# A four-layer decoder trunk on one core: the feed forward's gate and up by tokens in 512 columns, and all weight splits on VectorE

## The chip, the core and the metric

The kernel runs on one core of one Trainium2 chip. A core has TensorE (PE, matrix products into PSUM), VectorE (DVE), ScalarE (ACT), GpSimd (POOL) and SyncE (SP, which here issues the loads), each with its own instruction stream; they meet through semaphores. The metric is the device time of one execution in microseconds, the median of several runs.

## The reference

Input x has 256 tokens of width 1024, c is one conditioning vector. Four layers follow each other. Each has a token mixer (sliding window attention, gated linear attention, forgetting attention, sliding window again) and a feed forward of inner width 2816, both behind an RMS norm whose shift, scale and gate come from c:

```python
for i in range(DEPTH):                        # 4
    mod = silu(c) @ ada_w[i] + ada_b[i]       # 6 vectors of 1024
    sh1, sc1, g1, sh2, sc2, g2 = jnp.split(mod, 6, axis=-1)
    h = modulate(rmsnorm(x, norm_gain[i, 0]), sh1, sc1)
    x = x + g1[:, None, :] * mixer(h)
    h = modulate(rmsnorm(x, norm_gain[i, 1]), sh2, sc2)
    g, u = jnp.split(h @ ffn_w_gu[i], 2, axis=-1)
    x = x + g2[:, None, :] * ((silu(g) * u) @ ffn_w_down[i])
return rmsnorm(x, final_norm)
```

All data are float32. One pass over the weights, some 296 MB, is read from HBM.

## The kernel before

**Layout.** x, h and the inner activation lie with features on the 128 partitions and the 256 tokens along the free dimension: x is 8 tiles of 128 features, the inner activation 22 (FT). S is 256, P is 128, KT is 8, NB is 2 blocks of 128 tokens.

**Three products for one.** Products run in float32r, a shorter format at a higher pace. To keep float32's precision each operand is split in two parts, hi = round(v) and lo = v - hi, and `mm3` (L258) makes a product from three: hi x hi, hi x lo, lo x hi (L260, L261, L262). A weight's first part wh is a cast on ScalarE (L195), its second part wl a subtraction (L197) on VectorE, or on GpSimd for the pieces that `on_pool` lists. An activation is split in the same way by `split_hl` (L491: cast at L493, subtraction at L494).

**The stream of weights.** `Stream` (L76) holds all matrices in the order of use. Each is one load of 1 MB (a down weight 0.7 MB) into one of five raw buffers (RAW), issued on SP when the matrix five places ahead has been worked off and its readers are done. A "w" matrix is split in `cuts` pieces (four: 512 columns, or 352 of a down weight); an "a" matrix, a quarter of a modulation vector's matrix, is multiplied with silu(c) and summed on VectorE in two steps of 1024 columns (L217). The builder places this work between the products: `start_chunk` (L222) divides the pieces that are due by the ticks of the chunk, and each `tick` emits its share, up to two weights ahead (LOOK). The layer below fixes each engine's order when the program is built, by its own estimate of what is ready; at run time every engine then goes through its list in that order and stands still where the next instruction waits.

**Who splits.** `MIX_POOL`, `OUT_POOL` and `FFN_POOL` (L55, L62, L63) give one of a weight's four pieces to GpSimd in most stages, two in layer 2's mixer.

**The feed forward** (`ffn`, L1029). Gate and up: 22 weights a layer, each 128 gate columns beside 128 up columns, "by features": the weight is PE's stationary operand, h's 256 tokens stream by. A weight is a chunk of 16 x 3 = 48 products of 256 columns. The first chunk (`first_chunk`, L447) starts from x before the norm is known. Then ScalarE makes silu(g) (L1044), VectorE multiplies by u (L1045), ScalarE casts the result to ah (L493), GpSimd subtracts to al (L494). PSUM's "mm" banks (three) are used in turn, so PE can be two chunks ahead of the activation. Down: for each of 8 output tiles m two weights (11 tiles of depth each), 22 x 3 products of 256 columns into one accumulator; then `add_x` (L496) adds it to x, times the gate, on VectorE, and `x_done` (L400) prepares the next norm. Between the gate/up weights come four vectors' modulation matrices (16 loads; in layer 3 one vector's, 4 loads), between the down weights four loads more (not in layer 3).

Of the kernel before, what the change touches and what calls it, by code (L numbers as in the profile page):

```python
# [10 lines left out]
F32R = mybir.dt.float32r  # L11
# [6 lines left out]
P = 128  # L18
# [36 lines left out]
MIX_POOL = ((0,), (0,), (0, 1), (2,))  # L55
# [5 lines left out]
CUTS = (4, 4, 4)  # L61
OUT_POOL = (1,)  # L62
FFN_POOL = (3,)  # L63
# [12 lines left out]
class Stream:  # L76
    """Matrices in the order of use: each is loaded once; a weight is then split into two float32r
    parts, a modulation matrix multiplied with c. The work on them is cut into pieces, which the
    builder places between the products of the chunks before."""
# [19 lines left out]
    def piece(self):  # L99
        """Emit the next piece, unless it would run too far ahead."""  # L100
# [43 lines left out]
class Builder:  # L144
# [56 lines left out]
    def ada_pieces(self, it, raw):  # L201
        """Two tiles of 128 columns of c_act @ ada_w + ada_b."""
# [61 lines left out]
    def banks(self, split):  # L264
        """Two accumulators: in one bank, one after the other, or side by side in two."""
# [9 lines left out]
    def proj_feat(self, w, hs, split=None):  # L275
        """[cols, tokens]: weights stationary, two tiles of 128 columns."""
# [13 lines left out]
    def proj_tok(self, w, hs, split=None):  # L290
        """[tokens, 256 cols] for both blocks of tokens: activations stationary."""
# [13 lines left out]
    def stat_start(self, acc):  # L305
        """The means of squares, but for the last tile's."""
# [5 lines left out]
    def stat_end(self, acc=None):  # L312
        """1/sqrt(mean + eps) of each token: a column for each block of tokens."""
# [14 lines left out]
    def spread(self, y):  # L328
        """A row of the tokens' values in all partitions, in PSUM."""
# [6 lines left out]
    def rsqrt(self, y, ms):  # L336
        """y = (ms + eps) ** -0.5 by Newton steps, where another table is in use."""
# [27 lines left out]
    def next_norm(self, layer, sub):  # L365
        """Before the last sums into x: the modulation of the norm that follows."""
# [24 lines left out]
    def u_space(self, tag, dtype=F32):  # L391
        """The room of u, which is free between a sublayer's first chunk and the next norm."""
# [7 lines left out]
    def x_done(self, m, eng=None):  # L400
        """x's tile m is final: its squares, and its product with the gain in two parts."""
# [99 lines left out]
    def out_proj(self, layer, oh, ol, gate):  # L501
        """The mixer's last product, in two halves of its depth."""
# [179 lines left out]
    def first_chunks(self):  # L682
        """The first chunks of layer 0, k by k as the modulation comes in."""
# [72 lines left out]
    def few_cols(self, parts):  # L756
        """The 16 columns after a chunk's 256, as [16 cols, tokens] in PSUM."""
# [70 lines left out]
    def gla(self, layer, oh, ol, pool):  # L828
# [41 lines left out]
        def decay(h, li):  # L870
            """exp(-|b - b at the end of the even block| / 16) for every token."""
# [157 lines left out]
    def ffn(self, layer):  # L1029
        nc = self.nc  # L1030
        gate = self.mod[layer][:, 5 * KT:6 * KT]
        with self.tc.tile_pool(name=f"ffn{layer}", bufs=1, reuse_waits="tile") as pool:
            ah = self.t(pool, [P, FT, S], "ah", F32R)
# [278 lines left out]
```

## Time and profile before

Three runs took 1326.77 us (median), 1325.36 and 1332.42 us. The profiled execution's span, from the first to the last instruction, is 1324.8 us: 2.0 us under the median.

| stretch of the span | layer 0 | layer 1 | layer 2 | layer 3 |
|---|---|---|---|---|
| mixer, us | 157.4 | 136.7 | 129.1 | 99.2 |
| gate and up, us | 132.8 | 130.6 | 130.8 | 129.6 |
| down, us | 67.1 | 67.3 | 71.3 | 63.9 |

The rest, 9.0 us, is the last norm and the output. Over the span the loads move 224 GB/s; the busiest stage moves 299 GB/s with its 16 DMA engines busy 82% of the time.

How to read the lines that follow. A row of groups or of a line's instructions names line, engine, operation and operands as out<-in; "x600" is a count. A row of the timeline begins with the start in us and the duration in us. Products on PE are pipelined: a row's duration is longer than its share of the time, and the pace is the difference of two starts. In the table by stretches each engine has its busy time in us and, in brackets, its instructions. A row of waits has the sum in us, the number of waits and the longest. PE's weight loads stand apart as PEld. PEclk is the granted share of PE's clock.

### The profile page before, as it was taken

What the parts mean: (1) busy time and instruction counts of PE and PEld (TensorE: products, weight loads), DVE (VectorE), ACT (ScalarE), POOL (GpSimd) and SP (SyncE); (2) the same over time, 40 slices, a digit from 0 to 9 for tenths busy, and PEclk for the clock granted to TensorE, in tenths of its full rate; (3) what the DMA queues carried; (4) which work ended last, traced back from release to release, by engine and by line L of the source; (5) the groups of instructions that cost most, each with busy time, mean ns of one, the idle gap of its engine ahead of it and who ended that gap; (6) DMA issues with size and microseconds to landing.
All of it is one profiled execution on the core that took longest, in us unless ns stands there. A gap on an engine that the chain in (4) does not pass through costs nothing.

```text
span 1324.8 us, 25659 instructions
## 1 busy us (share of the span) xinstructions
PE 1240.9 (94%) x9748; PEld 1182.8 (89%) x9748; DVE 1036.2 (78%) x1959; ACT 756.3 (57%) x1770; POOL 593.3 (45%) x507
## 2 busy tenths in 40 slices
PE   3789899999998899999999999999999999999997
PEld 2666899999998889999999888999988878999997
DVE  5989999985889989897679557999757977744442
ACT  4466754544686656544556766644445667654443
POOL 6467355653435434554345423455434223444431
PEclk9989999999999999999999999999999999999999
DMA  7764679886745336887775443698767533565450
GB/s 313 254 224 159 258 256 333 343 284 238 283 165 180 136 131 243 334 321 266 247 288 182 178 164 123 259 342 321 252 223 284 197 128 119 200 223 201 161 180 33
DMA packets 44702, 298.89 MB, mean 226 GB/s; under 512 B 5169, under 2 KB 5329, under 8 KB 14242
## 3 DMA queue, kind: packets, MB, share of 16 engines
q1 hardware_dynamic: 43778, 295.53, 61.4%
q8 instruction: 76, 1.25, 0.4%
q10 hardware_dynamic: 432, 1.20, 0.2%
q0 software_dynamic: 368, 0.53, 0.2%
q14 instruction: 48, 0.39, 0.1%
HBM read 296.15 MB, written 1.05 MB: 224 GB/s over the span
## 4 chain that ended last, share of the span: by engine, by line
PE 50%; DVE 8%; DMA 3%; issue 2%; ACT 1%; POOL 0%; DVEq 0%; POOLq 0%; ACTq 0%; SPq 0%
PE mm L260 15%; PE mm L261 15%; PE mm L262 15%; DMA raw<-in_ada 3%; DVE wl L197 2%; PE o L551 1%; DVE hl L430 1%; DVE raw L217 1%; PE s L545 1%; DVE tk L435 1%; PE t L585 1%; PE s L544 1%; DVE x L497 1%; PE o L552 1%; DVE ul L419 0%
## 5 line engine op out<-in xcount | busy, mean ns | idle before, releaser
L195 ACT CAST wh<-raw 128x512 fp32r<-128x512 f32 (+1 forms) x816 | 430.2, 575 | 170.6 <-issue 85.0
L197 DVE TENSOR_TENSOR wl<-raw,wh 128x512 fp32r<-128x512 f32 (+2 forms) x600 | 439.6, 768 | 94.3 <-ACT wh L195 92.2
L197 POOL TENSOR_TENSOR wl<-raw,wh 128x512 fp32r<-128x512 f32 (+1 forms) x216 | 321.8, 1492 | 299.6 <-ACT wh L195 277.9
L260 PE MATMUL mm<-hh,wh 128*128 128x256 f32 x1504 | 429.3, 285 | 0.0
L262 PE MATMUL mm<-hh,wl 128*128 128x256 f32 x1504 | 426.5, 284 | 0.0
L261 PE MATMUL mm<-hl,wh 128*128 128x256 f32 x1504 | 426.3, 283 | 0.0
L217 DVE CUSTOM_DVE_ANT_0 raw<-raw,cact,const 128x1024 f32<-128x1024 f32 x174 | 289.7, 1684 | 81.4 <-DMA raw<-in_ada 79.5
L260 PEld LDWEIGHTS mm<-hh,wh 128*128 128x128 f32 x1504 | 289.1, 192 | 1.4 <-issue 1.4
L261 PEld LDWEIGHTS mm<-hl,wh 128*128 128x128 f32 x1504 | 289.2, 192 | 0.4 <-issue 0.3
L262 PEld LDWEIGHTS mm<-hh,wl 128*128 128x128 f32 x1504 | 289.0, 192 | 0.3 <-issue 0.3
L262 PE MATMUL mm<-ah,wl 128*128 128x256 f32 x704 | 200.5, 285 | 12.3 <-DVE wl L197 12.2
L494 POOL TENSOR_TENSOR al<-s,ah 128x256 fp32r<-128x256 f32 x88 | 105.5, 1200 | 227.0 <-ACT ah L493 216.4
L260 PE MATMUL mm<-ah,wh 128*128 128x256 f32 x704 | 200.3, 285 | 0.0
L261 PE MATMUL mm<-al,wh 128*128 128x256 f32 x704 | 199.4, 283 | 0.0
L262 PEld LDWEIGHTS mm<-ah,wl 128*128 128x128 f32 x704 | 133.9, 190 | 13.9 <-DVE wl L197 13.9
L261 PEld LDWEIGHTS mm<-al,wh 128*128 128x128 f32 x704 | 134.3, 191 | 0.0
L260 PEld LDWEIGHTS mm<-ah,wh 128*128 128x128 f32 x704 | 134.1, 190 | 0.0
L493 ACT CAST ah<-s 128x256 fp32r<-128x256 f32 x88 | 35.6, 407 | 125.5 <-DVE s L1045 124.5
L416 POOL TENSOR_TENSOR sq<-sq,sq 128x256 f32<-128x256 f32 x54 | 48.2, 892 | 100.2 <-ACT sq L405 99.0
L260 PE MATMUL mm<-wh,hh 128*128 128x256 f32 x240 | 73.4, 307 | 19.7 <-ACT hh L437 19.7
L405 ACT ACTIVATE sq<-x 128x256 f32<-128x256 f32 x72 | 29.6, 416 | 97.1 <-DVE x L497 95.2
L497 DVE SCALAR_TENSOR_TENSOR x<-mm,mod,x 128x256 f32<-128x256 f32 x96 | 45.7, 478 | 41.2 <-PE mm L262 40.8
(220 smaller groups left out, 2137.1 us busy)
## 6 DMA issues: line engine op xcount, KB each, us to landing
raw<-in_ada SPq DMA_DIRECT2D x96, 1024.0 KB, 6.1
raw<-in_gu SPq DMA_DIRECT2D x88, 1024.0 KB, 5.2
raw<-in_down SPq DMA_DIRECT2D x64, 704.0 KB, 4.9
raw<-in_swa_in SPq DMA_DIRECT2D x12, 1024.0 KB, 7.5
raw<-in_gla_in SPq DMA_DIRECT2D x11, 1024.0 KB, 5.2
raw<-in_fox_in SPq DMA_DIRECT2D x11, 1024.0 KB, 6.7
raw<-in_swa_o SPq DMA_DIRECT2D x8, 1024.0 KB, 4.8
raw<-in_gla_o SPq DMA_DIRECT2D x4, 1024.0 KB, 4.8
```

Source lines behind the costliest of these rows:

```text
L195: nc.scalar.copy(wh[:, sl], raw[:, sl])
L197: eng.tensor_tensor(out=wl[:, sl], in0=raw[:, sl], in1=wh[:, sl].bitcast(F32), op=ALU.subtract)
L217: nc.vector.tensor_tensor_reduce(out=w, in0=w, in1=self.cact, scale=1.0, scalar=b, op0=ALU.mult, op1=ALU.add, accum_out=col)
L260: nc.tensor.matmul(out, ah, bh, start=first, stop=False)
L261: nc.tensor.matmul(out, ah, bl, start=False, stop=False)
L262: nc.tensor.matmul(out, al, bh, start=False, stop=last)
L405: nc.scalar.activation(q, xm, AF.Square)
L416: (eng or nc.gpsimd).tensor_tensor(out=q, in0=self.acc, in1=q, op=ALU.add)
L430: nc.vector.scalar_tensor_tensor(out=hl[:, k], in0=tk, scalar=sh[:, k:k + 1], in1=hh[:, k].bitcast(F32), op0=ALU.add, op1=ALU.subtract)
L493: nc.scalar.copy(hi, src)
L494: (eng or nc.vector).tensor_tensor(out=lo, in0=src, in1=hi.bitcast(F32), op=ALU.subtract)
L497: self.nc.vector.scalar_tensor_tensor(out=self.x[:, m], in0=ps, scalar=gate[:, m:m + 1], in1=self.x[:, m], op0=ALU.mult, op1=ALU.add)
```

## The change

Constants: no piece goes to GpSimd, and a weight is cut in two (pieces of 1024 columns, 704 of a down weight).

```diff
-MIX_POOL = ((0,), (0,), (0, 1), (2,))
+MIX_POOL = ((), (), (), ())
...
-CUTS = (4, 4, 4)
-OUT_POOL = (1,)
-FFN_POOL = (3,)
+CUTS = (2, 2, 2)
+OUT_POOL = ()
+FFN_POOL = ()
```

Gate and up: the first two chunks of a layer stay by features (`gate_up_feat`, with their split on ScalarE and GpSimd). The other 20 weights are laid out anew on the host: two loads of 1 MB, each half of the depth, make a group of 256 gate and 256 up columns. A group goes "by tokens": h is stationary, 512 weight columns stream by, one PSUM bank for each block of 128 tokens. The result has tokens on the partitions, so four transposes on PE bring it back (`turn`); they stand in the program behind the second depth step of the next group, the last group's behind the fourth depth step of the down product.

```diff
+    def gate_up_tok(self, layer, g, pool, a, before):
+        nc = self.nc
+        hh, hl = self.hs
+        outs = [self.ps("s" if g % 2 == 0 else "mm") for _ in range(NB)]
+        for half in range(2):
+            w = self.st.get(f"g{layer}_{2 * g + half}")
+            wh, wl = (x.rearrange("p (k n) -> p k n", k=KT // 2) for x in w)
+            self.start_chunk(KT // 2)
+            for i in range(KT // 2):
+                k = half * (KT // 2) + i
+                for b in range(NB):
+                    sl = slice(b * P, (b + 1) * P)
+                    self.mm3(outs[b], hh[:, k, sl], hl[:, k, sl], wh[:, i], wl[:, i],
+                             k == 0, k == KT - 1)
+                if k == 1 and before is not None:
+                    before()
+                self.tick()
+        s = self.t(pool, [P, NB, 2 * P], "st", bufs=2)
+        for b in range(NB):
+            nc.scalar.activation(s[:, b], outs[b][:, :2 * P], AF.Silu)
+            nc.vector.tensor_tensor(out=s[:, b], in0=s[:, b], in1=outs[b][:, 2 * P:], op=ALU.mult)
+
+        def turn():
+            tp = self.ps("t")
+            for f in range(2):
+                for b in range(NB):
+                    nc.tensor.transpose(tp[:, f * S + b * P:f * S + (b + 1) * P],
+                                        s[:, b, f * P:(f + 1) * P], self.c("ident"))
+            tp = tp.rearrange("p (f n) -> p f n", f=2)
+            self.split_hl(tp, a[:, 2 * g:2 * g + 2, 0], a[:, 2 * g:2 * g + 2, 1])
+        return turn
```

Here `split_hl` has no engine named, so its subtraction, 512 columns from PSUM, is VectorE's.

Down: both parts of the activation lie side by side in one tile `a`, so the weight's first part multiplies both in one product of 512 columns, and its second part the first in one of 256. The accumulator is twice as wide, and its two halves are added to x one after the other.

```diff
-                        self.mm3(o, wh[:, k], wl[:, k], ah[:, kk], al[:, kk], kk == 0, kk == FT - 1)
+                        nc.tensor.matmul(o, wh[:, k], a[:, kk].rearrange("p e n -> p (e n)"),
+                                         start=kk == 0, stop=False)
+                        nc.tensor.matmul(o[:, S:], wl[:, k], a[:, kk, 0], start=False, stop=kk == FT - 1)
+                        if k == 3 and turn is not None:
+                            turn()
+                            turn = None
...
-                self.add_x(m, o, gate)
+                for e in range(2):
+                    self.add_x(m, o[:, e * S:(e + 1) * S], gate)
```

The rest of the diff is the host's layout of the gate/up weights and dropped comments.

More of the change, by code (lines that the diff above doesn't have):

```diff
@@ L1026, in gla, with gate_up_feat @@
         self.bg_rate = GLA_RATE[1]
+    def gate_up_feat(self, layer, j, pool, a):
+        nc = self.nc
+        s = self.t(pool, [P, S], "st", bufs=2)
+        if j == 0:
+            self.hs, ((gv, gc), (uv, uc)) = self.first_chunk(f"g{layer}_0")
+            nc.scalar.activation(s, gv, AF.Silu, bias=gc)
+            nc.vector.scalar_tensor_tensor(out=s, in0=uv, scalar=uc, in1=s, op0=ALU.add, op1=ALU.mult)
+        else:
+            g, u = self.proj_feat(self.st.get(f"g{layer}_{j}"), self.hs, "s")
+            nc.scalar.activation(s, g, AF.Silu)
+            nc.vector.tensor_tensor(out=s, in0=s, in1=u, op=ALU.mult)
+        self.split_hl(s, a[:, j, 0], a[:, j, 1], nc.gpsimd)
+    def gate_up_tok(self, layer, g, pool, a, before):
+        nc = self.nc
+        hh, hl = self.hs
[26 more added lines that the diff above has]
+        return turn
     def ffn(self, layer):
@@ L1032, in ffn @@
         with self.tc.tile_pool(name=f"ffn{layer}", bufs=1, reuse_waits="tile") as pool:
-            ah = self.t(pool, [P, FT, S], "ah", F32R)
-            al = self.t(pool, [P, FT, S], "al", F32R)
-            for j in range(FT):
-                s = self.t(pool, [P, S], "s", bufs=3)
-                if j == 0:
-                    hs, ((gv, gc), (uv, uc)) = self.first_chunk(f"g{layer}_0")
-                    nc.scalar.activation(s, gv, AF.Silu, bias=gc)
-                    nc.vector.scalar_tensor_tensor(out=s, in0=uv, scalar=uc, in1=s, op0=ALU.add,
-                                                   op1=ALU.mult)
-                else:
-                    g, u = self.proj_feat(self.st.get(f"g{layer}_{j}"), hs, "s" if j == 1 else None)
-                    nc.scalar.activation(s, g, AF.Silu)
-                    nc.vector.tensor_tensor(out=s, in0=s, in1=u, op=ALU.mult)
-                self.split_hl(s, ah[:, j], al[:, j], nc.gpsimd)
-                if layer == 0 and j == 2:
+            a = self.t(pool, [P, FT, 2, S], "a", F32R)
+            for j in range(2):
+                self.gate_up_feat(layer, j, pool, a)
+            turn = None
+            for g in range(1, FT // 2):
+                turn = self.gate_up_tok(layer, g, pool, a, turn)
+                if layer == 0 and g == 1:
                     self.late_loads()
-                elif layer == 0 and j == 9:
+                elif layer == 0 and g == 4:
                     self.late_consts()
@@ L1052, in ffn @@
             for m in range(KT):
-                o = self.ps("mm")[:, :S]
+                o = self.ps("mm")
                 for hf in range(2):
@@ L1059, in ffn @@
                         kk = hf * nk + k
-                        self.mm3(o, wh[:, k], wl[:, k], ah[:, kk], al[:, kk], kk == 0, kk == FT - 1)
+                        nc.tensor.matmul(o, wh[:, k], a[:, kk].rearrange("p e n -> p (e n)"),
[3 more added lines that the diff above has]
+                            turn()
+                            turn = None
                         if k % 2:
@@ L1237, in _layout @@
     a["ada"] = ada.reshape(DEPTH * 6, 4, 2, P, D).transpose(0, 1, 3, 2, 4).reshape(DEPTH * 6, 4, P, 2 * D)
-    gu = i["ffn_w_gu"].reshape(DEPTH, KT, P, 2, FT, P)
-    a["gu"] = gu.transpose(0, 4, 2, 1, 3, 5).reshape(DEPTH, FT, P, KT * 2 * P)
+    gu = i["ffn_w_gu"].reshape(DEPTH, KT, P, 2, FT, P)[:, :, :, :, :2]
+    gu = gu.transpose(0, 4, 2, 1, 3, 5).reshape(DEPTH, 2, P, KT * 2 * P)
+    gt = i["ffn_w_gu"].reshape(DEPTH, 2, KT // 2, P, 2, FT // 2, 2 * P)[:, :, :, :, :, 1:]
+    gt = gt.transpose(0, 5, 1, 3, 2, 4, 6).reshape(DEPTH, FT - 2, P, KT * 2 * P)
+    a["gu"] = np.concatenate([gu, gt], 1)
     dn = i["ffn_w_down"].reshape(DEPTH, 2, FT // 2, P, KT, P)
```

## The prediction

> **What bounds the kernel now.** I read the page's busy times and its chain first, then the busy times stretch by stretch, with the borders at the first product of each feed forward (first chunk), of each down product and of each mixer.
>
> ```profile
> PE 1240.9 (94%) x9748; PEld 1182.8 (89%) x9748; DVE 1036.2 (78%) x1959; ACT 756.3 (57%) x1770; POOL 593.3 (45%) x507
> ```
> ```profile
> PE 50%; DVE 8%; DMA 3%; issue 2%; ACT 1%; POOL 0%; DVEq 0%; POOLq 0%; ACTq 0%; SPq 0%
> ```
> ```profile
> core 0: us, PE busy (x) PEld busy (x) DVE busy (x) ACT busy (x) POOL busy (x), PEclk, DMA share, GB/s
> 0.00:157.40 157.40, 115.79 (x697) 93.37 (x698) 133.12 (x271) 94.11 (x231) 91.88 (x86) 0.97 0.65 245
> 157.40:290.20 132.80, 129.36 (x1070) 128.32 (x1069) 130.48 (x185) 68.86 (x152) 74.66 (x49) 1.00 0.82 299
> 290.20:357.30 67.10, 63.45 (x530) 62.84 (x529) 47.09 (x79) 34.18 (x82) 25.75 (x24) 1.00 0.74 259
> 357.30:494.00 136.70, 125.71 (x993) 121.24 (x992) 122.64 (x285) 94.49 (x200) 58.26 (x56) 0.99 0.45 159
> 494.00:624.60 130.60, 129.29 (x1070) 128.27 (x1069) 117.72 (x177) 67.88 (x146) 65.86 (x44) 1.00 0.78 294
> 624.60:691.90 67.30, 64.97 (x530) 64.55 (x529) 47.09 (x83) 34.58 (x83) 26.21 (x24) 0.97 0.73 254
> 691.90:821.00 129.10, 125.92 (x961) 114.81 (x960) 88.60 (x206) 93.08 (x241) 56.05 (x50) 1.00 0.48 167
> 821.00:951.80 130.80, 129.35 (x1070) 128.32 (x1069) 118.22 (x177) 67.82 (x147) 67.22 (x44) 1.00 0.79 293
> 951.80:1023.10 71.30, 65.02 (x531) 64.42 (x530) 47.23 (x83) 34.36 (x83) 26.13 (x24) 0.98 0.69 240
> 1023.10:1122.30 99.20, 97.68 (x698) 83.15 (x697) 84.15 (x235) 67.35 (x181) 27.71 (x47) 1.00 0.43 153
> 1122.30:1251.90 129.60, 128.79 (x1071) 128.30 (x1069) 72.59 (x130) 66.86 (x147) 53.82 (x45) 1.00 0.55 197
> ```
>
> Half of the chain is PE, and in the four gate/up stages (132.8, 130.6, 130.8, 129.6 us) PE is busy but for 1 to 3 us. VectorE (DVE) runs beside it and is nearly full in layer 0 (130.5 of 132.8 us), yet without stopping PE. The down stages lose 2 to 6 us each. So in the feed forwards a shorter PE stream is worth its full length, as long as VectorE keeps up; the waits show where it doesn't:
>
> ```profile
> ACT ah L493 <- DVE s L1045: 124.5, 62, 6.0
> ...
> DVE raw L217 <- DMA raw<-in_ada: 79.5, 24, 6.1
> ...
> PEld mm L262 <- DVE wl L197: 13.9, 8, 3.3
> ```
>
> PE itself waits only 13.9 us for split weights, all of it in products with wl, behind modulation loads that VectorE waited for. But ScalarE waits 124.5 us for VectorE's s: VectorE is late, and so far nobody on PE minds.
>
> **The pace of a product.** The next rows give start times of PE's products.
>
> ```profile
> 229.75 0.28 PE L260 MATMUL mm<-hh,wh 128*128 128x256 f32 x1
> ...
> 235.51 0.28 PE L260 MATMUL mm<-hh,wh 128*128 128x256 f32 x1
> ...
> 699.02 0.28 PE L260 MATMUL s<-wh,hh 128*128 128x272 f32 x1
> ...
> 703.52 0.29 PE L260 MATMUL s<-wh,hh 128*128 128x272 f32 x1
> ```
> ```profile
> 358.79 0.47 PE L309 MATMUL t<-const,sq 128*128 128x1 f32 x3
> 359.12 0.58 PE L322 MATMUL t<-const,sq 128*128 128x1 f32 x4
> ...
> 749.21 0.28 PE L262 MATMUL mm<-hh,wl 128*128 128x256 f32 x1
> 749.33 0.49 PE L585 MATMUL t<-const,pr 128*128 128x128 f32 x3
> 749.57 0.37 PE L260 MATMUL mm<-hh,wh 128*128 128x256 f32 x1
> 749.78 0.28 PE L261 MATMUL mm<-hl,wh 128*128 128x256 f32 x1
> ```
>
> A chunk's 48 products of 256 columns take 5.76 us: 120 ns each. Thirty-six products of 272 columns take 4.50 us: 125 ns each. One-column products go 0.33 us for three, 110 ns each: that is what a change of weights costs with nothing to stream, so a good part of the 120 ns is a load that a longer stream could hide. Three transposes between two products: from 749.21 to 749.78 are 570 ns where two products alone would take 240, so 330 ns, 110 ns a transpose.
>
> No product of 512 columns of this type is in the trace. Ends: if all 120 ns go by columns, 240 ns; if only the growth from 256 to 272 columns counts (5 ns for 16), 120 + 256 x 0.31 = 199 ns. The slope hangs on 5 ns and the proportional end on nothing being fixed, so I take the middle, a little to the long side: 222 ns.
>
> The Trainium skill, TensorE: Matmul & The Clock Gate, section Back-to-back issue gap, gives the spacing as N / 2.4 plus 2.5 ns, 216 ns at 512 columns. The same rule gives 109 ns at 256, where the trace shows 120, so it is short here by 11. By 216 the sum below would be about 15 us lower.
>
> **The change, part by part.**
>
> *Gate and up.* Of 22 weights a layer 20 go by tokens: 20 x 48 x 4 = 3840 products of 256 columns become 1920 of 512. Gain 1920 x (240 - 222) = 34.6 us (0 to 79 by the ends). Added on PE: four transposes for each of 10 groups in 4 layers, 160 x 0.110 = 17.6 us, all on the path, since PE is the bound. The rows above show one transpose alone to last 0.27 us (0.49 for three less two steps of 0.11); in the stream only its 0.11 counts. The loads stay the same in number, size and queue; a group now fills two PSUM banks at once, "mm" and "s" in turn, and "s" is otherwise idle there.
>
> The Trainium skill, same page, section Part 4: PE-mode transpose, speaks against this step: it gives about 275 ns for a transpose in a kernel. By that the 160 would cost 44 us, not 17.6, and the sum would lose all its gain; the trace's 110 ns in the stream of products contradicts it here.
>
> *Down.* Three products of 256 become one of 512 and one of 256, 704 times: 704 x 18 = 12.7 us (0 to 29). Each sum into x is now two steps of VectorE; inside the stage the next tile's products hide the second, at the end of a layer nothing does.
>
> ```profile
> L197 DVE TENSOR_TENSOR wl<-raw,wh x600: 507/679/4459, 17.6 to 1305.4; 128x512 fp32r<-128x512 f32 x101, 128x352 fp32r<-128x352 f32 x48, 128x544 fp32r<-128x544 f32 x1
> ```
> ```profile
> L217 DVE CUSTOM_DVE_ANT_0 raw<-raw,cact,const x174: 1256/1286/3396, 14.8 to 1229.0; 128x1024 f32<-128x1024 f32 x174
> ```
> ```profile
> L1045 DVE TENSOR_TENSOR s<-s,mm x80: 405/410/420, 184.3 to 1253.0; 128x256 f32<-128x256 f32 x80
> ```
> ```profile
> L497 DVE SCALAR_TENSOR_TENSOR x<-mm,mod,x x96: 467/479/486, 121.5 to 1316.1; 128x256 f32<-128x256 f32 x96
> ```
>
> These are min/median/max in ns. Four layer ends x 0.4 us (0.479 less an overlap of 0.08): +1.6 us.
>
> *The split on VectorE alone.* A piece of 512 costs 0.679 us, one of 352 0.507: 1.08 ns a column, so a piece of 1024 about 1.23 us. A weight costs VectorE 2.46 us, where it paid three pieces, 2.04 us, and GpSimd the fourth. But these prices are of undisturbed steps: the maxima (4459 and 3396 ns) are steps that run beside GpSimd, while L1045, which reads one input from PSUM, is never stretched (405 to 420). GpSimd loses its split pieces and nearly all L494 pieces, so most of the stretching goes. A group (two weights) in layers 0 to 2 then asks of VectorE: four pieces 4.92, 1.6 modulation matrices of two steps 1.6 x 2 x 1.29 = 4.1, two products with s 0.82, the new split from PSUM 0.41 + 256 x 1.08 ns = 0.69: 10.5 us, near 10 with the 0.08 us by which following steps overlap (0.68 at 593.97, below, and the next 0.60 later). PE needs 48 x 0.222 + 0.44 = 11.1 us. VectorE fits, with a tenth to spare; layer 3 has a quarter of the matrices. ScalarE has fewer, longer casts and no longer waits for s.
>
> *Waits removed and added.* A raw buffer is given back to SP when its last reader is done; GpSimd's late pieces no longer hold it, so modulation loads are issued sooner. I take half of PE's 13.9 us as gone: -6 us (0 to -13). The added wait is PE's own: the transposes need s, and behind them in PE's order stand the next group's products. They are placed after twelve products, 12 x 0.222 = 2.7 us after the group's end, the last group's after four pairs of the down product, 4 x (0.222 + 0.120) = 1.4 us. How late s is today, in layer 1:
>
> ```profile
> 590.72 0.38 ACT L1044 ACTIVATE s<-mm 128x256 f32<-128x256 f32 x1
> ```
> ```profile
> 593.97 0.68 DVE L197 TENSOR_TENSOR wl<-raw,wh 128x512 fp32r<-128x512 f32 x1
> 594.57 0.41 DVE L1045 TENSOR_TENSOR s<-s,mm 128x256 f32<-128x256 f32 x1
> ```
>
> VectorE ends s 4.3 us after ScalarE began it, held up by the pieces and matrix steps ahead of it. With the stretching gone and the load per group under PE's, I expect s about 2 to 2.5 us after the group's end: free in most groups, 0.1 us on average, and 1 us at each down stage: +7 us in all (0 to 48, second rival).
>
> *Mixers.* Pieces of 1.23 us stand longer in front of the attention steps, but are stretched less. VectorE was busy 133.1 of 157.4 us in layer 0. I put 0, within 6 us either way.
>
> Sum: -34.6 + 17.6 - 12.7 + 1.6 - 6 + 7 = -27.1 us. From the span of 1324.8 us that gives 1297.7; the median of the three runs is 2.0 us above the span, so **1300 us** (1299.7), 2.0% less.
>
> **Rivals.**
>
> *VectorE's lateness reaches PE (slower).* One mechanism: the transposes wait for s, with all of PE behind them. It decides from a delay of 2.7 us on. If s stays as late as the row at 590.72 shows, 4.3 us, thirty groups of layers 0 to 2 pay 1.6 us each, and their last ones 1.3 us more: 52 us in place of my 7, 1345 us. For it: the 124.5 us of ScalarE's waits. Against: the stretched steps are GpSimd's doing, and it falls silent. Chance 0.10.
>
> *Long products gain nothing (slower).* At 240 ns the 47.3 us of gain vanish and the transposes stay: 1347 us. For it: 272 columns cost more than 256. Against: a one-column product already costs 110. Chance 0.05.
>
> *VectorE becomes the bound.* It has a tenth to spare in three gate/up stages. If a group takes it 12 us (steps that wait for one another between transposes, cast and split), 30 groups cost 0.9 us each: 1327 us. The attention steps behind longer pieces could lose as much. For it: 130.5 of 132.8 us busy in layer 0. Against: those are stretched prices. Chance 0.12.
>
> *The weight load is nearly all of the fixed part.* At 205 ns a product, (222 - 205) x 2624 = 44.6 us more are gained: 1255 us. For it: the slope. Against: it rests on that alone. Chance 0.05.
>
> *Transposes stand alone in PE's stream.* At their full 0.27 us they cost 43 us in place of 17.6: 1325 us. Against: the three between 749.21 and 749.78. Chance 0.02. By the page's 275 ns the time would be the same 1326.
>
> **How the numbers follow.** The forecast's own case has the remaining 0.66. Its spread: 2624 products x 8 ns, 21 us either way, and the mixers' 6 us, about 1276 to 1324. About 0.5%, 6.6 us, is what a measurement of this kernel can tell from no change, so faster is below 1320 and slower above 1333. Faster: 0.61 of the forecast's case, the 0.05, and a third of the third rival, 0.70. Same: the forecast's upper end 0.05, half of the third rival, part of the last, 0.12. Slower: the first two and the rest, 0.18. The range runs from the forecast's lower end to the cheaper half of the first rival (a delay of 3.8 us in place of 4.3 gives 1330): 1272 to 1334. Outside lie the second and fourth rival and half of the first, 0.15, and tails.
>
> **What would show it.** Right: in the gate/up stages 512-column rows 216 to 228 ns apart; stages 3 to 5 us shorter; down stages near 63 us; VectorE's L197 pieces at about 1.2 us with short maxima, its total near 900 to 950 us though it does all the splitting; GpSimd far below its 593.3 us; transposes on PE with idle time before them under 10 us in all. Wrong: PE waiting for VectorE's s at the transposes by more than 1 us a group, 512-column rows 235 ns apart or more, or mixers longer by over 6 us.

## The result, and the profile after

| | before | after |
|---|---|---|
| time, median, us | 1329.60 (1325.36 to 1333.18, 4 runs) | 1290.78 (1287.15 to 1292.24, 4 runs) |
| profiled execution, us | 1326.77 | 1287.15 |
| its span, us | 1324.8 | 1285.4 |

The ratio of after to before is 0.9702, with a 95% interval from 0.9664 to 0.974: faster by 3.0%. The forecast was 1300 us, so the time came out 9 us lower, well inside the range. The working behind it did not come out as well. Of the ten executions of mix_off, an experiment further down, two were far slower than the others (1358.9 and 3007.6 us) and are left out of its figures.

First the page's line of busy times, then the table by stretches with the same borders (first product of each feed forward, of each down product, of each mixer).

```profile
PE 1223.3 (95%) x7284; PEld 1061.3 (83%) x7284; DVE 1029.2 (80%) x1839; ACT 719.4 (56%) x1323; POOL 200.5 (16%) x211
```
```profile
core 0: us, PE busy (x) PEld busy (x) DVE busy (x) ACT busy (x) POOL busy (x), PEclk, DMA share, GB/s
0.00:152.20 152.20, 112.55 (x695) 91.95 (x696) 132.59 (x264) 92.96 (x210) 82.16 (x75) 0.98 0.69 262
152.20:279.50 127.30, 126.70 (x627) 106.72 (x626) 114.37 (x168) 63.25 (x95) 6.21 (x6) 1.00 0.83 307
279.50:342.70 63.20, 62.59 (x358) 54.65 (x357) 50.62 (x72) 32.03 (x51) 7.81 (x6) 1.00 0.79 272
342.70:476.30 133.60, 125.84 (x991) 121.06 (x990) 115.09 (x271) 90.10 (x167) 36.54 (x39) 0.99 0.45 159
476.30:605.90 129.60, 128.01 (x627) 108.09 (x626) 114.41 (x168) 63.08 (x93) 6.35 (x4) 0.99 0.81 297
605.90:668.20 62.30, 62.30 (x358) 54.70 (x356) 49.80 (x70) 31.93 (x51) 7.83 (x6) 1.00 0.80 277
668.20:795.70 127.50, 125.83 (x960) 115.08 (x959) 87.89 (x204) 90.78 (x209) 16.18 (x21) 1.00 0.46 167
795.70:922.70 127.00, 126.64 (x627) 106.62 (x626) 115.27 (x170) 62.66 (x93) 4.84 (x4) 1.00 0.83 305
922.70:985.00 62.30, 62.30 (x358) 54.71 (x356) 48.57 (x68) 31.94 (x51) 7.82 (x6) 1.00 0.78 273
985.00:1083.80 98.80, 98.64 (x698) 83.62 (x697) 82.00 (x226) 66.20 (x162) 12.41 (x37) 1.00 0.43 150
1083.80:1212.20 128.40, 126.60 (x627) 106.63 (x626) 84.61 (x116) 64.01 (x93) 4.77 (x4) 1.00 0.57 202
1212.20:1276.00 63.80, 63.80 (x371) 56.21 (x370) 31.47 (x45) 27.97 (x47) 7.54 (x6) 1.00 0.32 106
```

Add up the stages of one kind and set them against the table of before. The mixers fell from 522.4 to 512.1 us (-10.3), gate and up from 523.8 to 512.3 (-11.5), down from 269.6 to 251.6 (-18.0); the end grew by 0.4 us. That is the whole 39.4 us of the span. The largest part lies in the down stages, where the long products save least, and a quarter lies in the mixers, whose products did not change at all. In the down stages of layers 1 to 3 PE is now busy throughout; VectorE makes every weight's second part and is still busy for fewer microseconds than before (1029.2 in place of 1036.2).

The pace of the new products, in gate and up (36 steps lie between the two rows) and in down (12 pairs):

```profile
812.03 0.39 PE L261 MATMUL mm<-wl,hh 128*128 128x512 f32 x1
...
820.19 0.39 PE L261 MATMUL mm<-wl,hh 128*128 128x512 f32 x1
```
```profile
929.64 0.40 PE L1100 MATMUL mm<-a,wh 128*128 128x512 f32 x1
929.87 0.28 PE L1102 MATMUL mm<-a,wl 128*128 128x256 f32 x1
...
933.85 0.40 PE L1100 MATMUL mm<-a,wh 128*128 128x512 f32 x1
```

A product of 512 columns takes (820.19 - 812.03) / 36 = 227 ns against 240 for two of 256. A pair in down takes 4.21 / 12 = 351 ns against 360 for three products. From 256 to 512 columns a product grows by 107 ns, so by a straight line through the two only 13 of the 120 ns were fixed.

The waits of VectorE for modulation loads and the new wait at the transposes, from VectorE's waits, from the rows of line 1071 and from PE's waits:

```profile
DVE st L1065 <- ACT st L1064: 35.5, 50, 2.7
...
DVE raw L217 <- DMA raw<-in_ada: 15.3, 9, 6.8
```
```profile
L1071 PE MATMUL t<-const,st x160: 269/272/331, 180.2 to 1214.1; 128*128 128x128 f32 x160
its engine sat idle before it (us, times) until:
  DVE st L1065: 1.5, 2
```
```profile
PEld t L1071 <- DVE st L1065: 0.9, 1, 0.9
...
PEld mm L262 <- DVE wl L197: 0.7, 1, 0.7
...
PE t L1071 <- DVE st L1065: 0.6, 1, 0.6
```

The loads' 79.5 us are 15.3. The 1.5 us at the transposes are a single wait that the rows of line 1071 count twice, once for the weight load (0.9) and once for the product (0.6): PE itself loses 0.6 us, at the start of layer 0's down stage. The 13.9 us before products with wl, which are a row of weight loads too, shrank to one wait of 0.7 us, and that one lies in a mixer.

### The profile page after: what moved, and what is told of

The parts are those of the page before. It is cut to its first block, busy times and chain, and to the rows that moved or that the text cites. A ratio compares the mean times of both kernels' runs of the same rounds, so it can differ in the third digit from the quotient of the medians.

```text
span 1285.4 us, 19492 instructions
## 1 busy us (share of the span) xinstructions
PE 1223.3 (95%) x7284; PEld 1061.3 (83%) x7284; DVE 1029.2 (80%) x1839; ACT 719.4 (56%) x1323; POOL 200.5 (16%) x211
## 4 chain that ended last, share of the span: by engine, by line
PE 83%; DVE 9%; ACT 3%; issue 2%; DMA 2%; POOL 1%; DVEq 0%; SPq 0%; POOLq 0%; ACTq 0%
PE mm L1100 13%; PE mm L260 12%; PE mm L261 11%; PE mm L262 11%; PE mm L1102 7%; PE s L260 6%; PE s L261 6%; PE s L262 6%; DVE raw L217 2%; DVE wl L197 2%; PE o L551 2%; PE t L1071 1%; PE s L545 1%; DMA raw<-in_ada 1%; PE t L585 1%
## 5 line engine op out<-in xcount | busy, mean ns | idle before, releaser
L197 DVE TENSOR_TENSOR wl<-raw,wh 128x1024 fp32r<-128x1024 f32 (+2 forms) x408 | 454.6, 1147 | 85.5 <-ACT wh L195 84.3
L195 ACT CAST wh<-raw 128x1024 fp32r<-128x1024 f32 (+2 forms) x408 | 376.5, 963 | 224.2 <-issue 105.9
L1100 PE MATMUL mm<-a,wh 128*128 128x512 f32 x704 | 248.8, 395 | 0.0
L217 DVE CUSTOM_DVE_ANT_0 raw<-raw,cact,const 128x1024 f32<-128x1024 f32 x174 | 230.0, 1337 | 15.3 <-DMA raw<-in_ada 15.3
L260 PE MATMUL mm<-wh,hh 128*128 128x512 f32 (+1 forms) x560 | 200.5, 358 | 20.1 <-ACT hh L437 20.1
L1102 PE MATMUL mm<-a,wl 128*128 128x256 f32 x704 | 199.5, 283 | 0.0
L262 PE MATMUL mm<-wh,hl 128*128 128x512 f32 (+1 forms) x560 | 195.5, 350 | 1.3 <-DVE hl L430 1.3
L261 PE MATMUL mm<-wl,hh 128*128 128x512 f32 (+1 forms) x560 | 195.4, 349 | 0.0
L260 PE MATMUL s<-wh,hh 128*128 128x512 f32 (+2 forms) x384 | 144.7, 378 | 2.9 <-ACT hh L437 2.9
L261 PE MATMUL s<-wl,hh 128*128 128x512 f32 (+2 forms) x384 | 143.0, 373 | 0.2 <-DVE wl L197 0.2
L262 PE MATMUL s<-wh,hl 128*128 128x512 f32 (+2 forms) x384 | 142.2, 374 | 0.0
L260 PEld LDWEIGHTS s<-wh,hh 128*128 128x128 f32 x384 | 72.5, 189 | 15.3 <-ACT hh L437 3.4
```

What stands on the lines that cost most here:

```text
L195: nc.scalar.copy(wh[:, sl], raw[:, sl])
L197: eng.tensor_tensor(out=wl[:, sl], in0=raw[:, sl], in1=wh[:, sl].bitcast(F32), op=ALU.subtract)
L217: nc.vector.tensor_tensor_reduce(out=w, in0=w, in1=self.cact, scale=1.0, scalar=b, op0=ALU.mult, op1=ALU.add, accum_out=col)
L260: nc.tensor.matmul(out, ah, bh, start=first, stop=False)
L261: nc.tensor.matmul(out, ah, bl, start=False, stop=False)
L262: nc.tensor.matmul(out, al, bh, start=False, stop=last)
```

## The experiments

Two theories stood against each other. P: the long products make the gain, as in the prediction's sum. S: the split without GpSimd makes it, because GpSimd's pieces hold up VectorE, the raw buffers and the products with wl. All times below are medians of several executions; the ratio is to the kernel before on the same chip, with its 95% interval. The table by stages comes from the one profiled execution of each kernel (sums over four layers, us). cuts4 and after_cut4_again are the same kernel, so their rows show what two executions differ by: 5 us in the mixers.

| kernel | time | ratio | mixers | gate/up | down |
|---|---|---|---|---|---|
| before | 1327 to 1330 | 1 | 522 | 524 | 270 |
| after | 1290.8 | 0.9702 (0.9664 to 0.974) | 512 | 512 | 252 |
| split_only | 1289.7 | 0.9722 (0.9693 to 0.975) | 513 | 519 | 252 |
| products_only | 1309.3 | 0.9864 (0.9838 to 0.989) | 526 | 520 | 251 |
| cuts4 | 1285.5 | 0.9683 (0.9656 to 0.971) | 512 | 512 | 251 |
| after_cut4_again | 1288.4 | 0.9714 (0.9693 to 0.9734) | 517 | 512 | 251 |
| down_256 | 1287.9 | 0.9701 (0.9678 to 0.9725) | 508 | 514 | 254 |
| cuts4_down256 | 1288.4 | 0.9696 (0.9672 to 0.972) | 512 | 512 | 254 |
| pool_off_4 | 1295.3 | 0.9747 (0.9727 to 0.9767) | 510 | 521 | 252 |
| al_dve | 1319.7 | 0.9927 (0.9906 to 0.9947) | 526 | 525 | 258 |
| mix_off | 1322.5 | 0.9959 (0.9934 to 0.9984) | 515 | 529 | 266 |
| ffn_off | 1305.5 | 0.9813 (0.9793 to 0.9834) | 524 | 518 | 252 |
| no_turn4 | 1266.9 | 0.9533 (0.9513 to 0.9554) | 511 | 495 | 249 |
| pool_copy | 1352.2 | 1.0195 (1.0171 to 1.022) | 543 | 528 | 270 |

### Each half of the change alone

split_only is the kernel before with the diff's constants (no piece on GpSimd, two pieces to a weight) and nothing else. products_only is the changed kernel with these constants put back.

> The kernel before with the split alone changed: no pieces on GpSimd, two pieces a weight; feed forward and its L494 subtraction on GpSimd as before. Theory P (as predicted: the long products bring most, PE's waits for late loads 6 us, the mixers nothing): about 6 us faster than before, 1322 to 1326, mixers unchanged. Theory S (the split's move off GpSimd brings most: the steps that GpSimd stretched on VectorE become short, so loads are issued sooner and the mixers' stalls shrink, while a product of 512 columns saves only 13 ns on two of 256): 22 to 28 us faster, 1300 to 1308; mixers about 10 us shorter, down stages about 13 us shorter in all.

> The changed feed forward with the split as before (four pieces, one or two of them on GpSimd). Theory P: the gain of the products stays, 1300 to 1308. Theory S: 29.6 us gained on long products less 18 for transposes is 11 us, 1316 to 1322, mixers and PE's waits in the down stages as before. The lateness rival: GpSimd stretches VectorE's steps again, s comes over 2.7 us after the group's end and PE waits for it at the transposes, 1 us or more a group in layers 0 to 2: 1335 to 1360, with idle time before the transposes of 30 us or more, where the changed kernel has 1.5.

split_only ran in 1289.7 us and products_only in 1309.3. The split alone gives as much as both together: P's 1322 to 1326 for it is off by more than 30 us, and S's own 1300 to 1308 by 10. Products_only lies between the two expectations and far from the 1335 to 1360 of VectorE's lateness, which falls: PE's own wait at the transposes is 3.6 us there. The two gains, 2.8% and 1.4%, do not add up to 3.0%: the table shows that both halves take nearly the same out of the down stages (17 and 19 us), and only the split takes 9 us out of the mixers. One execution could differ by 5 us there, but all kernels bear it out: the seven others with no weight piece on GpSimd have mixers of 508 to 517 us, and before, products_only, al_dve and ffn_off, which keep pieces in the mixers, 522 to 526.

### The size of the pieces, and the down product

```diff
-CUTS = (2, 2, 2)
+CUTS = (4, 4, 4)
```

> The changed kernel with four pieces a weight in place of two, all on VectorE. If GpSimd's absence is what counts, within 4 us of the changed kernel (1287 to 1295): the fixed part of 816 steps in place of 408 is VectorE's and ScalarE's, 0.07 us each, off PE's path. If the longer pieces matter by themselves, over 8 us slower (VectorE and ScalarE fuller) or faster (shorter steps in front of the attention).

down_256 puts the three products of 256 columns and the single sum into x back into down, in the changed kernel:

```diff
-                        nc.tensor.matmul(o, wh[:, k], a[:, kk].rearrange("p e n -> p (e n)"),
-                                         start=kk == 0, stop=False)
-                        nc.tensor.matmul(o[:, S:], wl[:, k], a[:, kk, 0], start=False, stop=kk == FT - 1)
+                        self.mm3(o[:, :S], wh[:, k], wl[:, k], a[:, kk, 0], a[:, kk, 1],
+                                 kk == 0, kk == FT - 1)
```

> The changed kernel with the down product as before: three products of 256 columns and one sum into x; everything else as changed. Theory P: the 512-column product there is worth 12.7 us less the second sum, so 1301 to 1305. Theory S: 704 x 6.5 ns (233 + 120.5 against 360) is 4.6 us less 1.6 for the second sums, so 1291 to 1296, and the stages stay free of PE's waits for wl.

> The changed kernel with four pieces to a weight, all on VectorE, and with the down product in three products of 256 columns as before. The two edits alone gave 1285.5 and 1287.9 us against 1290.8. If they add, 1281 to 1284 us; if the 512-column down product is worth its 4.6 us of pace and the run with it alone hid that behind something else, 1287 to 1291 us.

> The changed kernel with four pieces to a weight once more, on the same chip as the run beside it: 1284 to 1288 us. It gives the steps of the other run their counterpart with GpSimd silent, and a second look at how many half-clock spells an execution has: between 2 and 5 before the tail.

All four lie with the changed kernel, between 0.9683 and 0.9714, and their intervals overlap. So neither the size of a piece nor the form of the down product can be told apart by the time. Down_256 came out below both of its expectations, cuts4 1.5 us below the lower end of its first, and after_cut4_again 0.4 us above the range of its own, with seven spells of half clock where 2 to 5 were named. By the stages the 512-column down product is worth 0.9 us a layer (63.2 us with three products of 256 in each of layers 0 to 2, 62.3 in layers 1 and 2 of after), about 3 us in all once the longer end is taken off. No version with the whole computation beats the changed kernel beyond its interval.

### What the by-token form is worth with GpSimd out of the split

pool_off_4 is the kernel before with the three lists of GpSimd's pieces empty and four pieces to a weight.

> The kernel before, with all weight pieces on VectorE, still four to a weight (512 columns); the products are those of before. Theory S (GpSimd's silence is what counts, the size of the piece is not): as with two pieces to a weight, 1286 to 1293 us, mixers about 10 us shorter, down stages 62 to 64 us. If the larger piece carries a part, 1295 to 1310 us. Against the kernel with all of the change and four pieces (1285.5 us) this run shows what the 512-column products are worth once GpSimd is out of the split: 6 to 10 us by the pace of the products alone (227 ns against 240 in gate and up, 353 against 360 a triple in down, less 18 us of transposes), nothing by theory S in its plain form.

no_turn4 is cuts4 without the four transposes of a group; the split reads the gate and up result as it stands, so the transposition is left out of the computation:

```diff
-            tp = self.ps("t")
-            for f in range(2):
-                for b in range(NB):
-                    nc.tensor.transpose(tp[:, f * S + b * P:f * S + (b + 1) * P],
-                                        s[:, b, f * P:(f + 1) * P], self.c("ident"))
-            tp = tp.rearrange("p (f n) -> p f n", f=2)
+            tp = s
```

> The changed kernel with four pieces to a weight, all on VectorE, and without the four transposes of a group: the gate and up result goes to the split as it stands, so the transposition of the inner activation is left out of the computation. If the transposes stand wholly on PE's path, 160 of them at 110 to 115 ns are 18 us, and this runs in 1266 to 1269 us against 1285.5 with them. If they also made PE wait for the activation, or VectorE late, it falls below 1264 us. If something else sets the pace of gate and up (VectorE's pieces, the loads), it stays above 1275 us.

pool_off_4 came out at 1295.3 us: taking the pieces off GpSimd is worth 2.5% with no product changed. What the new products add on top of it is the step from 0.9747 to the two measurements of cuts4, 0.9683 and 0.9714: 4 to 9 us. With two pieces to a weight, as in the change itself, the times show none of it (split_only 0.9722, after 0.9702, with overlapping intervals). Pool_off_4 itself lies 2 us above theory S, at the foot of the range for a larger piece that carries a part; its interval overlaps that of split_only, so the larger piece is not shown to carry one. No_turn4 is 19 to 22 us faster than the two measurements of cuts4, and within the 1266 to 1269 us named for transposes that stand wholly on PE's path. One gate/up stage in cuts4 and in no_turn4, layer 1:

```profile
479.10:606.20 127.10, 126.24 (x627) 106.54 (x626) 116.11 (x211) 66.81 (x137) 4.32 (x4) 1.00 0.82 303
```
```profile
474.90:597.80 122.90, 122.04 (x591) 102.95 (x590) 113.89 (x209) 66.68 (x137) 4.28 (x4) 1.00 0.82 312
```

The stage is 4.2 us shorter without its 36 transposes (the last group's four stand in the down stage), 117 ns each: PE is what bounds gate and up, and the transposes give back most of what the long products save there.

### Why the down stages came free

al_dve leaves GpSimd its pieces in the kernel before and gives only the subtraction of the inner activation to VectorE:

```diff
-                self.split_hl(s, ah[:, j], al[:, j], nc.gpsimd)
+                self.split_hl(s, ah[:, j], al[:, j])
```

> The kernel before, with one edit: the second part of the inner activation (88 subtractions of 256 columns in gate and up) is made by VectorE and not by GpSimd. GpSimd keeps its weight pieces; cuts, products and layouts are those of before. Theory Q (GpSimd's queue): in gate and up GpSimd's weight pieces stand behind subtractions that wait for the activation, raw buffers come free late, and the down stages begin with their loads some 4 us behind: with the subtractions gone the down stages fall from 67, 67, 71 to 62 to 64 us, the mixers stay as they are, and the time is 1305 to 1313 us. Theory D (the 512-column down product, or the by-token gate and up, took the down stages' waits away in the kernel with the products alone): nothing changes here, 1323 to 1332 us, or slower, since VectorE has 88 more subtractions of 0.6 to 1.0 us.

mix_off empties `MIX_POOL` alone; ffn_off empties `OUT_POOL` and `FFN_POOL` and keeps `MIX_POOL`.

> The kernel before with GpSimd's pieces given to VectorE in the mixers' weights alone; GpSimd keeps a piece of each weight in gate and up and in down, and of the mixers' last product. Four pieces to a weight. If the mixers' gain is their own (GpSimd's pieces stretch VectorE's, and its steps stand behind them), mixers 0 to 2 are 8 to 13 us shorter in sum and the down stages stay at 67 to 71 us: 1315 to 1321 us. If the mixers only inherit what the feed forward's stages leave late, they stay within 3 us of before: 1324 to 1332 us.

> The kernel before with GpSimd's pieces given to VectorE in gate and up, in down and in the mixers' last product; in the mixers' own weights GpSimd keeps its pieces, and it keeps the subtraction of the inner activation. Four pieces to a weight. If the down stages' waits come from the pieces that GpSimd makes of the feed forward's weights, they fall to 62 to 64 us and the mixers stay: 1305 to 1313 us. If they come from the subtraction of the inner activation in GpSimd's queue alone, they stay at 65 us or more: 1318 to 1328 us. With the other kernel of this call the gains should add to that of the kernel with no piece on GpSimd, 34 us.

ffn_off came out where the pieces of the feed forward's weights were to be the cause. al_dve fell between its two expectations, and mix_off, at 1322.5 us, 1.5 us above the first of its own; its gate and up stages came out 5 us longer in the profiled execution. The down stages of layers 0 to 2, with the row of its kernel's VectorE waits behind them, first al_dve, then ffn_off:

```profile
290.80:354.90 64.10, 63.20 (x531) 62.80 (x530) 45.55 (x78) 34.48 (x82) 24.26 (x22) 1.00 0.75 260
622.20:687.50 65.30, 63.43 (x531) 63.02 (x530) 46.73 (x81) 34.54 (x83) 24.50 (x22) 1.00 0.75 261
950.10:1014.80 64.70, 63.25 (x531) 62.84 (x530) 46.94 (x81) 34.66 (x83) 26.10 (x22) 1.00 0.75 260
```
```profile
DVE raw L217 <- DMA raw<-in_ada: 67.8, 21, 5.7
```
```profile
290.10:352.70 62.60, 62.60 (x529) 62.60 (x529) 46.94 (x93) 34.80 (x82) 5.90 (x7) 1.00 0.75 270
...
617.30:680.00 62.70, 62.70 (x531) 62.70 (x530) 47.00 (x93) 34.71 (x82) 5.89 (x7) 1.00 0.76 271
...
940.00:1002.60 62.60, 62.60 (x530) 62.60 (x529) 46.92 (x93) 34.80 (x82) 5.89 (x7) 1.00 0.76 271
```
```profile
DVE raw L217 <- DMA raw<-in_ada: 25.1, 11, 5.2
```

With no piece of a feed-forward weight on GpSimd the three stages are 62.6 to 62.7 us, PE never stops, and VectorE waits 25.1 us for modulation loads in the whole kernel in place of 79.5. GpSimd still makes the subtraction of the inner activation there, so that one is not the cause by itself. With the subtraction gone and the pieces kept (al_dve) PE still loses time in each stage, and 12 of the 18 us are recovered. Read together: a raw buffer is free when its last piece is made, GpSimd's piece comes late, the next load is issued late, VectorE stands at a modulation step, and behind that step stands the second part that PE needs. GpSimd's other work makes its piece later still. The first link is in the waits of SyncE, which issues the loads, for a piece of GpSimd's; first before, then products_only:

```profile
SPq L182 <- POOL wl L197: 169.1, 103, 2.8
```
```profile
SPq L182 <- POOL wl L197: 78.5, 78, 1.2
```

In al_dve this wait is 108.8 us, and in ffn_off there is none. VectorE's wait for modulation loads goes down in the same order: 79.5, 67.8 and 31.8 us, and 25.1 in ffn_off. Products_only, which has the pieces but hardly any subtraction on GpSimd, recovers all of the down stages' loss; why its chain is shorter than al_dve's stays open. The chain is read from waits. In all these runs a buffer that comes late goes with a GpSimd step beside VectorE's, which makes VectorE late by another way (next section), and the two are not separated in the down stages.

In mix_off the mixers are 7.6 us shorter and in ffn_off 1.8 us longer than before, which speaks for a gain of the mixers' own, not inherited from the feed forward. That is one execution of each, and two executions of one kernel differed by 5 us there. The two gains, 0.4% and 1.9%, add up to pool_off_4's 2.5% within their intervals.

### Is it GpSimd's lateness, or its mere running?

In pool_copy VectorE makes every piece, as in pool_off_4. Where before gave a piece to GpSimd, GpSimd subtracts the piece's cast from itself into a scratch tile that nobody reads:

```diff
-            eng = nc.gpsimd if i in self.on_pool else nc.vector
-            eng.tensor_tensor(out=wl[:, sl], in0=raw[:, sl], in1=wh[:, sl].bitcast(F32),
-                              op=ALU.subtract)
+            nc.vector.tensor_tensor(out=wl[:, sl], in0=raw[:, sl], in1=wh[:, sl].bitcast(F32),
+                                    op=ALU.subtract)
+            if i in self.on_pool:
+                d = self.t(self.wpool, [P, 352], "unused", bufs=1)
+                for lo, hi in ((0, min(part, 352)), (352, part)):
+                    if hi > lo:
+                        w = wh[:, i * part + lo:i * part + hi].bitcast(F32)
+                        nc.gpsimd.tensor_tensor(out=d[:, :hi - lo], in0=w, in1=w, op=ALU.subtract)
```

> The kernel before with every weight piece on VectorE, four to a weight, and, where before gave a piece to GpSimd, GpSimd subtracts the piece's cast from itself into a scratch tile that nobody reads (352 and 160 columns one after the other, 352 of a down weight): added work, nothing left out. GpSimd is as busy as before and stands in its queue for the same casts; but no product waits for it, and no raw buffer. Theory C (GpSimd beside VectorE slows VectorE's own steps): VectorE's pieces are stretched again, modulation steps above 1.5 us in the mean, VectorE's sum of busy time near 1150 us, and the time comes back to 1310 to 1335 us. Theory W (what costs is that raw buffers and products wait for GpSimd's piece): 1293 to 1300 us, as with nothing on GpSimd (1295.3 us).

It ran in 1352.2 us, 57 us above pool_off_4 and 1.9% above the kernel before. The line of busy times and VectorE's two largest groups, first of pool_off_4, then of pool_copy (there line 196 is the piece and line 222 the modulation step):

```profile
PE 1231.3 (95%) x9748; PEld 1177.4 (91%) x9748; DVE 1053.4 (82%) x2175; ACT 754.2 (58%) x1770; POOL 260.9 (20%) x291
```
```profile
L197 DVE TENSOR_TENSOR wl<-raw,wh 128x512 fp32r<-128x512 f32 (+1 forms) x816 | 544.1, 712 | 91.2 <-ACT wh L195 89.1
L217 DVE CUSTOM_DVE_ANT_0 raw<-raw,cact,const 128x1024 f32<-128x1024 f32 x174 | 221.9, 1295 | 27.1 <-DMA raw<-in_ada 27.1
```
```profile
PE 1255.3 (93%) x9748; PEld 1193.2 (88%) x9748; DVE 1166.9 (86%) x2175; ACT 754.8 (56%) x1770; POOL 625.4 (46%) x659
```
```profile
L196 DVE TENSOR_TENSOR wl<-raw,wh 128x512 fp32r<-128x512 f32 (+1 forms) x816 | 618.2, 802 | 62.0 <-ACT wh L195 60.5
L222 DVE CUSTOM_DVE_ANT_0 raw<-raw,cact,const 128x1024 f32<-128x1024 f32 x174 | 254.1, 1480 | 25.6 <-DMA raw<-in_ada 25.6
```

The same 2175 steps of VectorE take 113.5 us longer when GpSimd runs beside them, with no raw buffer and no product waiting for GpSimd. Theory W is out as the only cause: its 1293 to 1300 us were missed by 52. Theory C gave the direction, and the time passed its upper end; a modulation step takes 1480 ns in the mean, just short of the 1.5 us that C named, and VectorE is busy for 1166.9 us where C had 1150. The size must not be carried back to the kernel before: the scratch steps are 368 in place of 216 and hold GpSimd for 357 us in place of 322, VectorE here makes the 216 pieces as well, and in nine places ScalarE's cast waits for a buffer that a scratch step still reads (15.1 us in all). GpSimd's own steps of the mixers also stand behind the scratch steps, and this run does not separate that from the stretching.

The down stages of layers 0 to 2 take 205.4 us in pool_copy, as long as before (205.7), although VectorE waits there only 19.5 us for modulation loads, where it waited 58.1. PE waits instead for the last inner activation, 7.4 of some 10 us, behind a VectorE that is late. So a late buffer is not needed for the down stages to lose this time.

## Why the prediction was right, and where it was wrong

The time was right because two errors cancelled: the long products were given too much, and the split without GpSimd too little. That is luck, and not a confirmed mechanism.

**A product of 512 columns at 222 ns: mis-sized.** It takes 227 ns in gate and up, and a pair in down 351 ns where the sum had 342. The 1920 long products of gate and up gain 1920 x 13 = 25 us in place of 34.6, the 704 in down 704 x 9 = 6 us by the pace and about 3 by the stages, in place of 12.7. The step that failed is the slope: 5 ns for 16 columns, or 0.31 ns a column, read off a difference near the resolution of the rows, where the step from 256 to 512 columns gives 107 / 256 = 0.42. The argument beside it failed with it: the 110 ns of a one-column product were taken for a part of the 120 that a longer stream could hide, but a product that streams 256 columns more takes 107 ns more, so nearly all of that was hidden at 256 columns already. I leaned towards the long end, and not far enough.

**Transposes at 0.110 us, all on the path: right.** 17.6 us in the sum; no_turn4 has 16.4 us less in its gate and up stages than cuts4 and 1.5 less in down, 18 in all, and 19 to 22 by the times. So gate and up's change of form is worth 7 or 8 us and down's 3, about 10 by the pace and the stages, 4 to 9 by the times, in place of 28.

**Second sums into x, +1.6 us: not contradicted.** The end behind the last down stage grew by 0.4 us, as priced; what the other three layer ends cost is not told apart from their mixers.

**Transposes waiting for s, +7 us: right in kind, too careful.** PE waits 0.6 us, once. VectorE keeps up, as the sum per group said, and the rival of VectorE's lateness reaching PE fell.

**Half of PE's 13.9 us of waits for wl: mis-sized.** All but 0.7 us went, and with them what follows a wait (last section). Down fell by 18.0 us, and by 17.5 in split_only, which has no long product. The reason given, raw buffers held by GpSimd's late pieces, agrees with ffn_off, where SyncE waits for no piece and PE never stops in these stages. Pool_copy shows that GpSimd's steps beside VectorE's can cost the down stages as much, so which of the two weighs more in the kernel before stays open.

**Mixers 0, within 6 us: wrong.** They fell by 10.3 us. The prediction had the fact in hand, steps stretched beside GpSimd up to 4459 ns, and used it only for the gate/up sum. pool_copy shows that it works in the mixers too: they are 33 us longer than pool_off_4's.

**VectorE's total of 900 to 950 us: wrong.** It is 1029.2 us. Lines 197 and 217 together fell from 729.3 to 684.6 us, first before, then after:

```profile
L197 DVE TENSOR_TENSOR wl<-raw,wh 128x512 fp32r<-128x512 f32 (+2 forms) x600 | 439.6, 768 | 94.3 <-ACT wh L195 92.2
...
L217 DVE CUSTOM_DVE_ANT_0 raw<-raw,cact,const 128x1024 f32<-128x1024 f32 x174 | 289.7, 1684 | 81.4 <-DMA raw<-in_ada 79.5
```
```profile
L197 DVE TENSOR_TENSOR wl<-raw,wh 128x1024 fp32r<-128x1024 f32 (+2 forms) x408 | 454.6, 1147 | 85.5 <-ACT wh L195 84.3
L217 DVE CUSTOM_DVE_ANT_0 raw<-raw,cact,const 128x1024 f32<-128x1024 f32 x174 | 230.0, 1337 | 15.3 <-DMA raw<-in_ada 15.3
```

The mean of a modulation step came down from 1684 ns, but not to the undisturbed 1286: 26 of the 174 still run beside a step that GpSimd keeps, at 1673 ns in the mean. The new split from PSUM and 32 more sums into x came on top. The prediction shows no working for its 900 to 950.

**Its signs.** The pace of 227 ns, the down stages near 63 us and the short waits at the transposes came as named. The gate and up stages are 5.5, 1.0, 3.8 and 1.2 us shorter, where 3 to 5 were named, and the longest piece on VectorE still takes 3404 ns.

## What to carry to other kernels

Before giving a second engine a share of a job, compare VectorE's total with and without the share: here 216 pieces cost GpSimd 322 us, and taking them back cost VectorE 17 us (1036.2 to 1053.4), because its other steps ran faster (the modulation steps went from 289.7 to 221.9 us). When a wait of the bounding engine lies at the end of a chain that begins with a late buffer, price the whole wait as gone if the buffer's holder goes, and look at every stage that the holder touches, not only the one that is being changed. Measure the pace of a longer product as two rows far apart; a slope from a 6% longer one is no basis for a 100% longer one.

## What the runs showed of the hardware

**PE's granted clock halves in spells of 3.41 us, most of them behind a wait.** Before, in layer 2's down stage, PE waits 3.13 us for a second part and then runs more slowly. The rows of PE's timeline, then two windows:

```profile
998.19 0.39 PE L262 MATMUL mm<-ah,wl 128*128 128x256 f32 x1 [3.13 <-DVE wl L197]
...
999.01 0.41 PE L260 MATMUL mm<-ah,wh 128*128 128x256 f32 x1
...
1001.57 0.41 PE L260 MATMUL mm<-ah,wh 128*128 128x256 f32 x1
```
```profile
994.50:998.40 3.90, 0.77 (x6) 0.57 (x5) 2.39 (x5) 0.67 (x2) 0.11 (x1) 1.00 0.28 114
998.40:1001.81 3.41, 3.41 (x18) 3.41 (x18) 3.41 (x6) 2.46 (x7) 2.35 (x2) 0.51 0.31 74
```

Between 999.01 and 1001.57 twelve products take 213 ns each, and 120 outside. So the spell costs about 1.5 us on top of the wait: sixteen products fill it, and each takes 93 ns more. The profiled execution before has five such spells ahead of its end, one of them double, the one after four. The five begin at 83.7, 114.4, 377.2, 667.4 and 998.4 us, whole multiples of 3.413 us apart (9, 77, 85 and 97). Where a wait falls on this grid counts, and not its length alone: PE's waits of 2.66 us up to 333.70 and of 2.52 us up to 983.04 had no spell behind them, one of 2.15 us up to 666.79 had.

The mean granted clock was 0.987 over twelve runs of before, 0.994 over four of pool_off_4 on the same chip and 0.980 over four of pool_copy on another: at most 0.7% of the time in the first comparison and about 1.5% between the last two hang on it, on top of the waits themselves, and less where a spell falls on a stretch in which PE waits anyway. Equal runs differ in the same way: of thirteen runs of before on one chip the one with a clock of 0.995 took 1318.89 us, one with 0.985 took 1333.08.

In after a spell followed a stretch in which PE was busy for 2.61 of 3.60 us:

```profile
477.80:481.40 3.60, 2.61 (x23) 2.41 (x22) 2.92 (x6) 1.45 (x5) 1.62 (x1) 1.00 0.66 262
481.40:484.80 3.40, 3.40 (x18) 3.40 (x18) 1.29 (x2) 1.64 (x4) 0.00 (x0) 0.50 0.00 0
```

The spell at 365.4 us of after even follows 3.40 us (362.0 to 365.4) in which PE never stood idle, with products of 16 rows in place of 128 among them. How little work brings on a spell is not shown.

The Trainium skill, TensorE: Matmul & The Clock Gate, section Part 1: The HAM clock gate (the "warmup" mystery), gives half rate after at least one idle window of about 3.4 us, in windows that run freely. The half rate and the 3.41 us agree with this trace, and the grid agrees with windows that run freely; the idle window does not, since here PE was busy for most of the stretch that preceded a spell.

**VectorE beside GpSimd.** Sorted by whether a GpSimd step runs at the same time (for more than 50 ns), the 174 modulation steps of before fall in two groups: 54 without one take 1278 ns in the mean and at most 1289, 120 beside one take 1867 in the mean and up to 3396. In pool_copy the two means are 1276 and 1582 ns (58 and 116 steps), in after 1278 and 1673 (148 and 26). So no step is stretched without a GpSimd step beside it, though not every step beside one is. The mean over all pieces of 512 and 352 columns rises from 712 ns in pool_off_4 to 802 in pool_copy, while the product with s, one input of which lies in PSUM, was never stretched (405 to 420 ns before). The Trainium skill, SBUF — State Buffer, section Who interferes with whom, says that a VectorE step with two inputs in SBUF contends with a GpSimd step that reads SBUF, and one with at most one such input, outside the two-port modes, does not; these rows agree.
